# Attention scores of two heads in the two row halves of TensorE, and one operand split for a whole pair

## The chip, the cores and the metric

The kernel runs on one core of one Trainium2 chip. Its time is device microseconds of one execution. The program is one launch: all inputs lie in the chip's memory, and the output goes back there.

## What is computed

Two layers of a decoder trunk over 256 tokens of width 1024, in float32. Each layer first mixes: 12 self-attention heads and 4 heads that attend to 256 memory tokens, all of width 64, share one input projection and one output projection. Layer 0 adds a learned forgetting term to the scores, layer 1 a distance term. Then each layer runs a gated feed-forward block of 2816 columns.

```
for i in range(DEPTH):                       # DEPTH = 2
    xn = rms_norm(h, norm_mix[i]);  mn = rms_norm(mem, norm_mem[i])
    mk, mv = split(mn @ w_mem_kv[i])
    q, k, v, (f_logit), qm = split(xn @ w_in[i])
    self_out = softmax(q k^T / 8 + bias, causal) v      # 12 heads
    mem_out  = softmax(qm mk^T / 8) mv                  # 4 heads
    h = h + concat(self_out, mem_out) @ w_out[i]
    gu = rms_norm(h, norm_ffn[i]) @ w_gate_up[i]
    h = h + (silu(gu[..., :D_FF]) * gu[..., D_FF:]) @ w_down[i]
return rms_norm(h, norm_final)
```

With 256 tokens the block-sparse attention of layer 1 has a single block, so it is plain causal attention there.

## The kernel before

**Products.** Every float32 operand of a product is split into two parts, `hi` (a copy rounded to the matmul's input type, by ScalarE) and `lo` (what the copy lost, a subtraction by VectorE). A product of two such operands is three matmuls: hi·hi, lo·hi and hi·lo (`prod`, line 320). The weights come from memory as one stream of units on SyncE's queue; `split` (line 215) makes `hi` and `lo` of each half unit, a copy of 128x1024 on ScalarE (L227) and a subtraction on VectorE (L230), five half units ahead of their use, into seven buffers of each.

**The mixer** (line 470) computes the values of all heads, then three groups of query and key columns (`qk_ps`, two pairs of heads in each), with the memory heads' projection (`qm_ps`, and in layer 0 also the memory keys and values) ahead of the second group. A pair of heads is one tile of 128 partitions: head 0 in partitions 0 to 63, head 1 in 64 to 127 (`HOME`). Each pair's attention is a generator (`attend`, line 394), and `step` (line 464) moves all active ones on by a stage between pieces of projection: scores (`s_s`, or `s_m` for memory heads), softmax, transposes of the probabilities (`pT`), and the product with the values (`o_s`, `o_m`). TensorE and SyncE run in the order in which this is written. VectorE, ScalarE and GpSimd are ordered by a scheduler, in which the softmax has a raised priority (`URGENT`).

**Scores before.** A head has 64 rows only, so the two parts of an operand are stacked in the 128 rows. `split_queries` (line 378) writes for head a its `hi` into the head's own 64 partitions and its `lo` into the other 64. `split_keys` (line 386) writes `hi` of the keys into both halves, and `lo` into the own half, with zeros in the other (`no_lo`, line 334, on GpSimd). One matmul then gives hi·hi + lo·hi and a second hi·lo. So there are two matmuls of 256 columns for each head and each block of 128 queries, 8 for a pair. The cost is in the preparation: for a self pair 6 copies of 64x256 on ScalarE (L381, L389, L390), 2 subtractions on GpSimd and 2 on VectorE (L383, L392), and 2 zero fills. For two memory pairs the keys take 8 copies and 4 subtractions, and the queries 4 and 4. Of the two heads of a pair GpSimd subtracts for head 0 and VectorE for head 1.

**Softmax.** The maxima read the scores in their PSUM bank (L420 for memory heads, L417 for self heads, which writes the biased scores into the tile `p_s`), ScalarE takes the exponentials (L427; for memory heads straight from the bank, so the bank stays taken until then), VectorE the reciprocals and the scaling (L428, L431). The probabilities and their transposes share one tag of three buffers, `probs`. PSUM has eight banks, all of one tag.

**The value products** `o_s` and `o_m` (line 446) write head 0 to output partitions 0 to 63 and head 1 to 64 to 127: each head uses one half of TensorE's columns. They run in plain float32.

Of the kernel before, what the change touches and what calls it, by code (L numbers as in the profile page):

```python
# [141 lines left out]
def trunk(ctx: ExitStack, tc: tile.TileContext, plan, stream, x, gains, norm_final, square, mem, out):  # L142
# [23 lines left out]
    mem_t = [ap.tile([P, 2, 512], F32, tag="probs", name=f"mem{t}", bufs=3).rearrange("p a s -> p (a s)") for t in range(NT)]  # L166
# [176 lines left out]
    def mem_kv(i):  # L343
# [24 lines left out]
        for p in range(HM // 2):  # L368
            split_keys(mks[p], mk[:, p])
# [6 lines left out]
    ENG = (nc.gpsimd, nc.vector)  # L376

    def split_queries(dst, q):

        for a in range(2):  # L380
            nc.scalar.activation(dst[HOME[a], a], q[HOME[a]], AF.Copy)  # L381
        for a in range(2):
            r = ENG[a].tensor_sub(dst[HOME[1 - a], a], q[HOME[a]], dst[HOME[a], a].bitcast(F32))  # L383
        return r

    def split_keys(dst, k):

        for a in range(2):
            nc.scalar.activation(dst[HOME[a], a, :S], k[HOME[a]], AF.Copy)  # L389
            nc.scalar.activation(dst[HOME[1 - a], a, :S], k[HOME[a]], AF.Copy)  # L390
        for a in range(2):
            ENG[a].tensor_sub(dst[HOME[a], a, S:], k[HOME[a]], dst[HOME[a], a, :S].bitcast(F32))  # L392

    def attend(name, xq, xk, vt, h0, idle, bias, dst, kt):
# [10 lines left out]
        for a in range(2):  # L405
# [5 lines left out]
        pr = ap.tile([P, 2, 512], F32, tag="probs", name=f"p_{name}", bufs=3)  # L411
# [27 lines left out]
        pT = ap.tile([P, 2, 512], F32, tag="probs", name=f"pT_{name}", bufs=3)  # L439
# [30 lines left out]
    def mixer(i, xs, rs):  # L470
# [76 lines left out]
        def memory_heads():  # L547
# [15 lines left out]
            nc.vector.tensor_mul(qm, qb.t.rearrange("p (a s) -> p a s", a=2), rsb[:, 0:1, :].to_broadcast([P, 2, S]))  # L563
            for p in range(HM // 2):
                xq = ap.tile([P, 2, S], F32R, tag="work", name=f"xqm{i}{p}", bufs=WORK_BUFS)
                mem_done[i] = split_queries(xq, qm[:, p]).ins
                active.append(attend(f"m{i}{p}", xq, mks[p], mvs, 2 * p, IDLE_MEM[i] + p, None, hT, 6 + p))

        for g in range(3):
# [18 lines left out]
            for a in range(2):  # L588
# [9 lines left out]
                active.append(attend(f"s{i}{p}", xq, xk, vsb, 2 * p, idle, bias, hT, p))  # L598
# [46 lines left out]
    def ffn(i, xs, late):  # L645
# [5 lines left out]
        def gu(c, kk):  # L651
# [13 lines left out]
            if first:  # L665
                rsb.append(spread(rs, f"f{i}", (1.0,), "f")[:, 0])
# [156 lines left out]
```

## Time and profile before

| | us |
|---|---|
| median of 3 runs | 621.79 (621.36 to 622.78) |
| the profiled execution | 621.42 |
| its span | 619.6 |
| TensorE busy in the span | 606.8 |
| VectorE busy | 452.7 |
| ScalarE busy | 393.2 |
| GpSimd busy | 63.4 |

The granted clock of TensorE was 0.998 of full speed over the span. The span is the part of an execution between its first and last instruction; some 1.8 us lie around it. The profile has one line for nearly every matmul, since all of them are issued by one helper (L183), so matmuls are told apart by the tile they write. A matmul's record lasts longer than the distance to the next one's start, because they are pipelined: what a matmul costs is read from start to start.

### The profile page before, as it was taken

What the parts mean: (1) busy time and instruction counts of PE and PEld (TensorE: products, weight loads), DVE (VectorE), ACT (ScalarE), POOL (GpSimd) and SP (SyncE); (2) the same over time, 40 slices, a digit from 0 to 9 for tenths busy, and PEclk for the clock granted to TensorE, in tenths of its full rate; (3) what the DMA queues carried; (4) which work ended last, traced back from release to release, by engine and by line L of the source; (5) the groups of instructions that cost most, each with busy time, mean ns of one, the idle gap of its engine ahead of it and who ended that gap; (6) DMA issues with size and microseconds to landing.
All of it is one profiled execution on the core that took longest, in us unless ns stands there. A gap on an engine that the chain in (4) does not pass through costs nothing.

```text
span 619.6 us, 9546 instructions
## 1 busy us (share of the span) xinstructions
PE 606.8 (98%) x3634; PEld 533.0 (86%) x3634; DVE 452.7 (73%) x815; ACT 393.2 (63%) x736; POOL 63.4 (10%) x90
## 2 busy tenths in 40 slices
PE   9999899999999999999999999999999999999995
PEld 6999888788888888888899998877888888888884
DVE  5677999687676776668675589986866766667664
ACT  6889788485555555557467589776755555555542
POOL 2032112055000000000011032110000000000000
PEclk9999999999999999999999999999999999999999
DMA  8977452335544554556355731332445555456301
GB/s 349 422 283 278 165 179 95 135 137 204 199 172 179 197 204 181 177 190 227 126 200 191 272 137 69 136 136 103 170 177 197 205 195 178 177 197 205 136 1 68
DMA packets 16774, 112.31 MB, mean 181 GB/s; under 512 B 1996, under 2 KB 2008, under 8 KB 4312
## 3 DMA queue, kind: packets, MB, share of 16 engines
q1 hardware_dynamic: 16440, 111.42, 49.0%
q8 instruction: 28, 0.46, 0.3%
q10 hardware_dynamic: 288, 0.29, 0.1%
q14 instruction: 18, 0.15, 0.1%
HBM read 110.64 MB, written 1.06 MB: 180 GB/s over the span
## 4 chain that ended last, share of the span: by engine, by line
PE 88%; DVE 5%; ACT 4%; issue 2%; POOL 0%; POOLq 0%; DVEq 0%; ACTq 0%
PE gu L183 40%; PE d_acc L183 18%; PE qk_ps L183 8%; PE o_acc L183 7%; PE v_ps L183 6%; DVE lo L230 2%; PE s_s L183 1%; ACT hi L227 1%; PE pT_s L438 1%; PE o_s L183 1%; PE mv_ps L183 1%; PE qm_ps L183 1%; PE mk_ps L183 1%; PE warm_ps L183 1%; DVE p_m L431 1%
## 5 line engine op out<-in xcount | busy, mean ns | idle before, releaser
L230 DVE TENSOR_TENSOR lo<-raw,hi 128x1024 fp32r<-128x1024 f32 (+3 forms) x201 | 239.7, 1198 | 67.0 <-ACT hi L227 62.1
L227 ACT ACTIVATE hi<-raw 128x1024 fp32r<-128x1024 f32 (+3 forms) x201 | 206.5, 1035 | 71.3 <-PE d_acc L183 46.8
L183 PE MATMUL gu<-x_ffn,hi 128*128 128x512 f32 x704 | 177.4, 392 | 0.0
L183 PEld LDWEIGHTS gu<-x_ffn,hi 128*128 128x128 f32 x704 | 126.3, 189 | 22.2
L183 PE MATMUL d_acc<-hi,h 128*128 128x512 f32 x348 | 107.1, 389 | 0.0
L183 PEld LDWEIGHTS gu<-x_ffn,lo 128*128 128x128 f32 x704 | 96.7, 190 | 8.1 <-ACT x_ffn L251 1.0
L183 PE MATMUL gu<-x_ffn,lo 128*128 128x256 f32 x704 | 100.5, 284 | 0.1
L183 PEld LDWEIGHTS d_acc<-hi,h 128*128 128x128 f32 x348 | 65.3, 188 | 13.6
L183 PE MATMUL qk_ps<-x_x,hi 128*128 128x256 f32 x384 | 72.4, 284 | 2.1 <-ACT p_m L427 2.1
L183 PE MATMUL d_acc<-lo,h 128*128 128x512 f32 x174 | 67.7, 389 | 0.0
L183 PEld LDWEIGHTS qk_ps<-x_x,hi 128*128 128x128 f32 x384 | 61.0, 191 | 3.3 <-ACT p_m L427 2.5
L183 PE MATMUL qk_ps<-x_x,lo 128*128 128x256 f32 x192 | 54.3, 283 | 0.0
L672 ACT ACTIVATE gate<-gu 128x256 f32<-128x256 f32 x44 | 16.9, 384 | 57.6 <-PE gu L183 57.6
L672 ACT ACTIVATE up<-gu 128x256 f32<-128x256 f32 x44 | 16.9, 385 | 39.7 <-PE gu L183 39.5
L183 PE MATMUL o_acc<-hi,x_hT 128*128 128x512 f32 x128 | 41.6, 404 | 0.3 <-DVE x_hT L249 0.3
L183 PEld LDWEIGHTS d_acc<-lo,h 128*128 128x128 f32 x174 | 32.7, 188 | 6.8
L673 DVE TENSOR_TENSOR gate<-gu,gate 128x256 f32<-128x256 f32 x44 | 18.7, 424 | 25.6 <-ACT gate L672 25.5
L183 PEld LDWEIGHTS qk_ps<-x_x,lo 128*128 128x128 f32 x192 | 36.8, 191 | 0.0
L673 DVE TENSOR_TENSOR up<-gu,up 128x256 f32<-128x256 f32 x44 | 18.7, 424 | 24.6 <-ACT up L672 24.6
L183 PE MATMUL v_ps<-hi,x_x 128*128 128x384 f32 (+1 forms) x128 | 33.1, 339 | 0.0
L183 PEld LDWEIGHTS o_acc<-hi,x_hT 128*128 128x128 f32 x128 | 22.9, 188 | 5.9 <-DVE x_hT L249 1.0
L427 ACT ACTIVATE p_s<-p_s,nmax_s 128x128 f32<-128x128 f32 (+1 forms) x48 | 21.3, 445 | 9.8 <-DVE nmax_s L417 9.7
(152 smaller groups left out, 752.2 us busy)
## 6 DMA issues: line engine op xcount, KB each, us to landing
raw<-in_stream SPq DMA_DIRECT2D x94, 1024.0 KB, 4.8
raw<-in_stream SPq DMA_DIRECT2D x3, 1036.0 KB, 7.9
raw<-in_stream SPq DMA_DIRECT2D x4, 768.0 KB, 4.5
fk<-fd SPq DMA_DIRECT2D x3, 512.0 KB, 7.5
raw<-in_stream SPq DMA_DIRECT2D x2, 518.0 KB, 4.4
h<-in_x SPq DMA_DIRECT2D x2, 512.0 KB, 11.9
mem<-in_mem SPq DMA_DIRECT2D x2, 512.0 KB, 12.5
gfin<-in_norm_final SPq DMA_DIRECT2D x1, 512.0 KB, 3.6
```

Source lines behind the costliest of these rows:

```text
L183: nc.tensor.matmul(o, lhsT, rhs, start=self.fresh, stop=stop, skip_group_check=True)
L227: nc.scalar.activation(hi[:, c0:c1], src[:, c0:c1], AF.Copy)
L230: nc.vector.tensor_sub(lo[:, c0:c1], src[:, c0:c1], hi[:, c0:c1].bitcast(F32))
L427: nc.scalar.activation(pr[:, a, c], src, AF.Exp, bias=nmax[:, a, j], scale=scale, accum_out=total[:, a, j])
L431: nc.vector.tensor_scalar_mul(pr[:, a, c], pr[:, a, c], rc[:, a, qt:qt + 1])
L438: nc.tensor.transpose(tb[a].t[:, n * P:(n + 1) * P], pr[:, a, c:c + P], ident)
L672: nc.scalar.activation(v[:, 1], b[s].t[:, S:], AF.Copy)
L673: nc.vector.tensor_add(v[:, 0], b[s].t[:, :S], v[:, 1])
```

## The change

**Scores.** The query and key operands of a pair are now one `hi` tile and one `lo` tile of all 128 partitions, each head in its own 64. Three matmuls (hi·hi, lo·hi, hi·lo) for each head and block of queries take the head's 64 partitions alone, so each uses one half of TensorE's rows; the two heads stand alternately, and write to two banks. A pair has 12 matmuls of 256 columns where it had 8.

**Splits.** `split_queries`, `split_keys` and `no_lo` are gone. `split_ps` does a self pair's queries and keys together: one copy of 128x512 on ScalarE (L248) and one subtraction of 128x512 on VectorE (L249), into a tile `xp`. The two memory pairs' queries (`xm`) and keys (`mks`) take one copy and one subtraction each. GpSimd has no part in them.

**Buffers.** `probs` has four buffers instead of three. `xm` takes a buffer of the tag `pair` where the `xqm` tiles were in `work`. The feed-forward's spread of the norm factors shares the tag of the mixer's.

```diff
-    mem_t = [ap.tile([P, 2, 512], F32, tag="probs", name=f"mem{t}", bufs=3)...
+    mem_t = [ap.tile([P, 2, 512], F32, tag="probs", name=f"mem{t}", bufs=4)...
@@ split_ps
-            nc.vector.tensor_sub(lo, ps, hi.bitcast(F32))
+            return nc.vector.tensor_sub(lo, ps, hi.bitcast(F32))
@@
-    mks = [cp.tile([P, 2, 2 * S], F32R, name=f"mk{p}") for p in range(HM // 2)]
+    mks = cp.tile([P, 2, HM // 2, S], F32R, name="mks")
@@ mem_kv
-        for p in range(HM // 2):
-            split_keys(mks[p], mk[:, p])
+        split_ps(mks[:, 0], mks[:, 1], mk)
@@ removed: no_lo, ENG, split_queries, split_keys
@@ attend
-        for a in range(2):
-            for qt in range(NT):
-                o, q = sb[a].t[:, qt * S:(qt + 1) * S], slice(qt * P, (qt + 1) * P)
-                sb[a].mm(o, xq[:, a, q], xk[:, a, :S])
-                sb[a].mm(o, xq[:, a, q], xk[:, a, S:], stop=True)
+        for qt in range(NT):
+            o, q = slice(qt * S, (qt + 1) * S), slice(qt * P, (qt + 1) * P)
+            for n, (st, mv) in enumerate(((xq[0], xk[0]), (xq[1], xk[0]), (xq[0], xk[1]))):
+                for a in range(2):
+                    sb[a].mm(sb[a].t[:, o], st[HOME[a], q], mv[HOME[a]], stop=n == 2)
@@ attend: pr and pT
-..., tag="probs", ..., bufs=3)
+..., tag="probs", ..., bufs=4)
@@ memory_heads
+            xm = ap.tile([P, 2, HM // 2, S], F32R, tag="pair", name=f"xm{i}", bufs=PAIR_BUFS)
+            mem_done[i] = split_ps(xm[:, 0], xm[:, 1], qm).ins
             for p in range(HM // 2):
-                xq = ap.tile([P, 2, S], F32R, tag="work", name=f"xqm{i}{p}", bufs=WORK_BUFS)
-                mem_done[i] = split_queries(xq, qm[:, p]).ins
@@ mixer
-                xq = ap.tile([P, 2, S], F32R, tag="work", name=f"xq{i}{p}", bufs=WORK_BUFS)
-                xk = ap.tile([P, 2, 2 * S], F32R, tag="pair", name=f"xk{i}{p}", bufs=PAIR_BUFS)
-                no_lo(xk)
-                split_queries(xq, qk[:, 0])
-                split_keys(xk, qk[:, 1])
+                xp = ap.tile([P, 2, 2, S], F32R, tag="pair", name=f"xp{i}{p}", bufs=PAIR_BUFS)
+                split_ps(xp[:, 0], xp[:, 1], qk)
@@ ffn
-                rsb.append(spread(rs, f"f{i}", (1.0,), "f")[:, 0])
+                rsb.append(spread(rs, f"f{i}", (1.0,), "x")[:, 0])
```

**Where it moves instructions.** TensorE's order of blocks is the same in both kernels: each block of scores stands between the same neighbours. On ScalarE in layer 0, from the memory keys to the memory queries, before (`mk_87` is the second memory pair's keys, `xqm_742` and `xqm_747` the two pairs' queries, `hi` the weights' copies):

```order
L389 ACTIVATE mk_87<-mk_662 64x256
L390 ACTIVATE mk_87<-mk_662 64x256
L389 ACTIVATE mk_87<-mk_662 64x256
L390 ACTIVATE mk_87<-mk_662 64x256
L227 ACTIVATE hi_0_712<-raw_432 128x1024
L227 ACTIVATE hi_2_754<-raw_432 128x1024
L227 ACTIVATE hi_0_784<-raw_555 128x1024
L381 ACTIVATE xqm_742<-qm_740 64x256 x2
L381 ACTIVATE xqm_747<-qm_740 64x256 x2
```

and after (`mks` is the copy of all memory keys, `xm` that of all memory queries):

```order
L227 ACTIVATE hi_0_675<-raw_427 128x1024
L248 ACTIVATE mks<-mk_635 128x512
L227 ACTIVATE hi_2_710<-raw_427 128x1024
L227 ACTIVATE hi_0_740<-raw_528 128x1024
L248 ACTIVATE xm_705<-qm_703 128x512
L227 ACTIVATE hi_2_800<-raw_528 128x1024
L227 ACTIVATE hi_0_897<-raw_600 128x1024
```

The copies of small tiles between the weights' copies have become one for the keys and one for the queries, and one weights' copy more stands ahead of the keys.

On VectorE in layer 0, from the last weights' subtraction ahead of the memory queries to the first memory pair's maxima, before:

```order
L230 TENSOR_TENSOR lo_0_713<-raw_432,hi_0_712 128x1024
L563 TENSOR_TENSOR qm_740<-qm_ps_681,rsb_x_479 128x512
L230 TENSOR_TENSOR lo_2_755<-raw_432,hi_2_754 128x1024
L383 TENSOR_TENSOR xqm_742<-qm_740,xqm_742 64x256
L383 TENSOR_TENSOR xqm_747<-qm_740,xqm_747 64x256
L230 TENSOR_TENSOR lo_0_785<-raw_555,hi_0_784 128x1024
L230 TENSOR_TENSOR lo_2_841<-raw_555,hi_2_840 128x1024
L539 TENSOR_TENSOR bias_868<-fk,sq 128x256
L539 TENSOR_TENSOR fk<-fk,sq 128x2x128 x2
L420 TENSOR_REDUCE nmax_m_822<-s_m_0_812 128x1 x2
L420 TENSOR_REDUCE nmax_m_822<-s_m_1_813 128x1 x2
```

and after:

```order
L230 TENSOR_TENSOR lo_2_711<-raw_427,hi_2_710 128x1024
L540 TENSOR_TENSOR qm_703<-qm_ps_644,rsb_x_474 128x512
L230 TENSOR_TENSOR lo_0_741<-raw_528,hi_0_740 128x1024
L249 TENSOR_TENSOR xm_705<-qm_703,xm_705 128x512
L230 TENSOR_TENSOR lo_2_801<-raw_528,hi_2_800 128x1024
L516 TENSOR_TENSOR bias_828<-fk,sq 128x256
L516 TENSOR_TENSOR fk<-fk,sq 128x2x128 x4
L230 TENSOR_TENSOR lo_0_898<-raw_600,hi_0_897 128x1024
L397 TENSOR_REDUCE nmax_m_782<-s_m_0_768 128x1 x2
L397 TENSOR_REDUCE nmax_m_782<-s_m_1_769 128x1 x2
```

The two `xqm` subtractions have become one of `xm`. The weights' subtractions stand one place earlier throughout (`lo_2_711` of after is `lo_2_755` of before, and so on), so that the one of `raw_627`, the next row of before, which followed the maxima, is now ahead of them (`lo_0_898`), with four mask additions (`fk`) instead of two.

On VectorE in layer 1, the scaling of the second memory pair's probabilities (`p_m`, L431 before, L408 after), which the transposes `pT_m` wait for, before:

```order
L428 RECIPROCAL rc_m_3996<-total_m_3995 128x2
L591 TENSOR_TENSOR qk_4078<-qk_ps_3835,rsb_x_3729 128x512
L431 TENSOR_SCALAR p_m_3990<-p_m_3990,rc_m_3996 128x256 x2
L428 RECIPROCAL rc_m_3996<-total_m_3995 128x2
L230 TENSOR_TENSOR lo_1_4113<-raw_3696,hi_1_4112 128x1024
L431 TENSOR_SCALAR p_m_3990<-p_m_3990,rc_m_3996 128x256 x2
L417 ISA p_s_4048,nmax_s_4047<-s_s_0_4037,fk 128x128
L417 ISA nmax_s_4047 128x1
L417 ISA p_s_4048,nmax_s_4047<-s_s_0_4037,fk 128x256
```

and after:

```order
L405 RECIPROCAL rc_m_3913<-total_m_3912 128x2
L394 ISA p_s_3969,nmax_s_3968<-s_s_0_3954,fk 128x128
L394 ISA nmax_s_3968 128x1
L408 TENSOR_SCALAR p_m_3907<-p_m_3907,rc_m_3913 128x256 x2
L394 ISA p_s_3969,nmax_s_3968<-s_s_0_3954,fk 128x256
L394 ISA nmax_s_3968 128x1
L394 ISA p_s_3969,nmax_s_3968<-s_s_1_3955,fk 128x128
L394 ISA nmax_s_3968 128x1
L405 RECIPROCAL rc_m_3913<-total_m_3912 128x2
L394 ISA p_s_3969,nmax_s_3968<-s_s_1_3955,fk 128x256
L394 ISA nmax_s_3968 128x1
L408 TENSOR_SCALAR p_m_3907<-p_m_3907,rc_m_3913 128x256 x2
```

Before, a weights' subtraction stood between the two scalings of `p_m`; now the four biased maxima of the next self pair (`p_s`) stand between and ahead of them, and the weights' subtraction has gone to another place.

## Rows read from the trace of the kernel before

**Rows 1.** The page's line of busy times: microseconds, share of the span and number of instructions of each engine.

```profile
PE 606.8 (98%) x3634; PEld 533.0 (86%) x3634; DVE 452.7 (73%) x815; ACT 393.2 (63%) x736; POOL 63.4 (10%) x90
```

**Rows 2.** TensorE's timeline around its four long waits in the mixers, two rows each: start, us, the instruction, how many are merged, and in brackets the idle time before it with what ended it.

```profile
60.03 0.28 PE L183 MATMUL qk_ps<-x_x,hi 128*128 128x256 f32 x1
61.16 0.51 PE L183 MATMUL s_m<-mk,xqm 128*128 128x256 f32 x2 [0.85 <-POOL xqm L383]
...
71.25 0.61 PE L438 MATMUL pT_m<-sq,p_m 128*128 128x128 f32 x4
73.04 0.38 PE L183 MATMUL qk_ps<-x_x,hi 128*128 128x256 f32 x1 [1.18 <-ACT p_m L427]
...
73.74 0.28 PE L183 MATMUL qk_ps<-x_x,hi 128*128 128x256 f32 x1
74.89 0.39 PE L183 MATMUL qk_ps<-x_x,hi 128*128 128x256 f32 x1 [0.88 <-ACT p_m L427]
...
377.44 0.60 PE L438 MATMUL pT_m<-sq,p_m 128*128 128x128 f32 x4
379.18 0.63 PE L438 MATMUL pT_m<-sq,p_m 128*128 128x128 f32 x4 [1.14 <-DVE nmax_s L417]
```

**Rows 3.** Busy time by stretch. Columns: stretch and its length, then busy us (and instructions) of PE, PEld, DVE, ACT and POOL, the granted clock, DMA share and GB/s. The stretches: layer 0 from the first pairs' split to the end of the memory queries' projection, layer 0 from the first scores to the last long wait, layer 1 likewise.

```profile
36.60:54.40 17.80, 17.80 (x148) 17.21 (x147) 14.40 (x17) 16.55 (x30) 5.02 (x5) 1.00 0.57 214
...
60.20:75.00 14.80, 11.90 (x96) 11.32 (x96) 14.74 (x46) 10.48 (x31) 3.01 (x6) 1.00 0.58 224
...
364.20:379.60 15.40, 14.27 (x122) 14.06 (x121) 15.22 (x48) 12.98 (x39) 3.50 (x7) 1.00 0.44 159
```

**Rows 4.** The chain that ended last, in order of time (start, us, engine and line), in layer 0 from 55 to 75 us and in layer 1 around 376 us.

```profile
55.59 0.42 ACT mk L389
...
56.47 1.07 ACT hi L227
...
57.56 1.23 DVE lo L230
58.79 0.60 DVE qm L563
...
60.55 0.72 DVE xqm L383
...
65.67 1.33 DVE nmax_m L420 x4
67.00 1.13 DVE lo L230
...
73.86 0.99 ACT p_m L427 x4
...
375.81 0.97 DVE lo L230
...
376.86 1.62 DVE p_m L431 x2
```

**Rows 5.** Groups by line, shapes kept apart: busy us, mean ns of one, idle before. The last row is from the view of the tile `p_m`: shortest, median and longest ns of one.

```profile
L381 ACT ACTIVATE xq<-qk 64x256 fp32r<-64x256 f32 x24 | 10.0, 415 | 4.1 <-DVE qk L591 3.7
L389 ACT ACTIVATE xk<-qk 64x256 fp32r<-64x256 f32 x24 | 10.0, 416 | 0.4
L383 DVE TENSOR_TENSOR xq<-qk,xq 64x256 fp32r<-64x256 f32 x12 | 8.1, 678 | 1.5 <-ACT xq L381 1.2
L392 DVE TENSOR_TENSOR xk<-qk,xk 64x256 fp32r<-64x256 f32 x12 | 5.8, 481 | 1.2 <-ACT xk L389 0.9
L383 DVE TENSOR_TENSOR xqm<-qm,xqm 64x256 fp32r<-64x256 f32 x4 | 3.4, 896 | 0.1
L591 DVE TENSOR_TENSOR qk<-qk_ps,rsb_x 128x512 f32<-128x512 f32 x12 | 8.0, 679 | 1.6 <-ACT rsb_x L283 1.6
L442 ACT ACTIVATE pT_m<-pT_m 128x512 f32<-128x512 f32 x4 | 2.3, 576 | 0.0
L431 DVE TENSOR_SCALAR p_m<-p_m,rc_m x16: 333/350/873, 68.4 to 377.6; 128x256 f32<-128x256 f32 x16
```

**Rows 6.** The same chain where it runs through TensorE without a wait in layer 0: start, us, tile, matmuls. The rows at 82.73 and 92.31 follow a block of `o_m` or `o_s`, the other two don't.

```profile
78.19 2.87 PE qk_ps L183 x24
...
82.73 3.07 PE qk_ps L183 x24
...
92.31 1.14 PE s_s L183 x8
...
101.27 0.95 PE s_s L183 x8
```

**Rows 7.** TensorE's timeline around `F_ps` (a float32 product in one tile: four records, two of 256 columns and two of 128) and around one `o_m` block (eight records of 256 columns, four for each head). `128*128`, `128*12`, `128*64` are the rows and columns of the array in use.

```profile
41.39 0.28 PE L183 MATMUL mv_ps<-lo,x_mem 128*128 128x256 f32 x1
41.60 0.82 PE L183 MATMUL F_ps<-sq,lf 128*12 128x256 f32 x4
42.35 0.38 PE L183 MATMUL mk_ps<-x_mem,hi 128*128 128x256 f32 x1
...
81.64 0.44 PE L183 MATMUL o_m<-pT_m,mv 128*64 128x256 f32 x2
...
82.66 0.39 PE L183 MATMUL qk_ps<-x_x,hi 128*128 128x256 f32 x1
82.89 0.28 PE L183 MATMUL qk_ps<-x_x,lo 128*128 128x256 f32 x1
```

More of the change, by code (lines that the diff above doesn't have):

```diff
@@ L163, in trunk @@
     nc.gpsimd.memset(minus_half, -0.5)
-    mem_t = [ap.tile([P, 2, 512], F32, tag="probs", name=f"mem{t}", bufs=3).rearrange("p a s -> p (a s)") for t in range(NT)]
+    mem_t = [ap.tile([P, 2, 512], F32, tag="probs", name=f"mem{t}", bufs=4).rearrange("p a s -> p (a s)") for t in range(NT)]
     def load_x():
@@ L373, in mem_kv @@
         yield
[L376 to L392, printed above, removed]
     def attend(name, xq, xk, vt, h0, idle, bias, dst, kt):
@@ L404, in attend @@
         sb = [bank(f"s_{name}_{a}") for a in range(2)]
-        for a in range(2):
-            for qt in range(NT):
-                o, q = sb[a].t[:, qt * S:(qt + 1) * S], slice(qt * P, (qt + 1) * P)
-                sb[a].mm(o, xq[:, a, q], xk[:, a, :S])
-                sb[a].mm(o, xq[:, a, q], xk[:, a, S:], stop=True)
+        for qt in range(NT):
[3 more added lines that the diff above has]
+                    sb[a].mm(sb[a].t[:, o], st[HOME[a], q], mv[HOME[a]], stop=n == 2)
         nmax = sp.tile([P, 2, NT], F32, tag="nmax", name=f"nmax_{name}")
-        pr = ap.tile([P, 2, 512], F32, tag="probs", name=f"p_{name}", bufs=3)
+        pr = ap.tile([P, 2, 512], F32, tag="probs", name=f"p_{name}", bufs=4)
         with tc.high_priority(offset=URGENT):
@@ L438, in attend @@
                 nc.tensor.transpose(tb[a].t[:, n * P:(n + 1) * P], pr[:, a, c:c + P], ident)
-        pT = ap.tile([P, 2, 512], F32, tag="probs", name=f"pT_{name}", bufs=3)
+        pT = ap.tile([P, 2, 512], F32, tag="probs", name=f"pT_{name}", bufs=4)
         width = len(blocks) * P
@@ L563, in memory_heads @@
             nc.vector.tensor_mul(qm, qb.t.rearrange("p (a s) -> p a s", a=2), rsb[:, 0:1, :].to_broadcast([P, 2, S]))
+            xm = ap.tile([P, 2, HM // 2, S], F32R, tag="pair", name=f"xm{i}", bufs=PAIR_BUFS)
+            mem_done[i] = split_ps(xm[:, 0], xm[:, 1], qm).ins
             for p in range(HM // 2):
-                xq = ap.tile([P, 2, S], F32R, tag="work", name=f"xqm{i}{p}", bufs=WORK_BUFS)
-                mem_done[i] = split_queries(xq, qm[:, p]).ins
-                active.append(attend(f"m{i}{p}", xq, mks[p], mvs, 2 * p, IDLE_MEM[i] + p, None, hT, 6 + p))
+                active.append(attend(f"m{i}{p}", (xm[:, 0, p], xm[:, 1, p]), (mks[:, 0, p], mks[:, 1, p]), mvs, 2 * p,
+                                     IDLE_MEM[i] + p, None, hT, 6 + p))
         for g in range(3):
@@ L591, in mixer @@
                 nc.vector.tensor_mul(qk.rearrange("p a s -> p (a s)"), kb[a].t, rsb.rearrange("p a s -> p (a s)"))
-                xq = ap.tile([P, 2, S], F32R, tag="work", name=f"xq{i}{p}", bufs=WORK_BUFS)
-                xk = ap.tile([P, 2, 2 * S], F32R, tag="pair", name=f"xk{i}{p}", bufs=PAIR_BUFS)
-                no_lo(xk)
-                split_queries(xq, qk[:, 0])
-                split_keys(xk, qk[:, 1])
+                xp = ap.tile([P, 2, 2, S], F32R, tag="pair", name=f"xp{i}{p}", bufs=PAIR_BUFS)
+                split_ps(xp[:, 0], xp[:, 1], qk)
                 idle = a + IDLE[i][g]
-                active.append(attend(f"s{i}{p}", xq, xk, vsb, 2 * p, idle, bias, hT, p))
+                active.append(attend(f"s{i}{p}", (xp[:, 0, 0], xp[:, 1, 0]), (xp[:, 0, 1], xp[:, 1, 1]), vsb, 2 * p, idle, bias, hT, p))
         acc = [[bank(f"o_acc{i}{t}{c}") for c in range(2)] for t in range(NT)]
@@ L772, in trunk @@
         nc.gpsimd.memset(warm, 0.0)
-        for mk in mks:
-            no_lo(mk)
         wb = bank("warm_ps")
```

2 lines of the change are left out of this document (removed).

## The prediction

> **What bounds the kernel now.** I read the busy line first: TensorE works in 98% of the span, the next engine, VectorE, in 73% [rows 1]. So what changes TensorE's stream, or its waits, changes the time; work taken from other engines counts only where TensorE waits for it. Next come TensorE's waits. In both mixers together it waits long four times, and from start to start each costs a little more than the bracket says: in layer 0 the scores `s_m` start 1.13 us after the matmul before, where 0.12 is usual, a loss of 1.0; the projection after `pT_m` starts 1.8 us after a group of four transposes that takes 0.44, a loss of 1.35; its next bank costs 1.15 − 0.12 = 1.03; in layer 1 the second half of `pT_m` starts 1.74 after the first, a loss of 1.3 [rows 2]. Sum 4.7 us. Behind them, by the stretches, is VectorE: busy 14.74 of 14.80 us in layer 0 and 15.22 of 15.40 in layer 1, while before that, from 36.6 to 54.4, ScalarE is the fuller one, 16.55 of 17.80 [rows 3]. The chain says the same: the small copies of the memory keys (L389) end at 56.45 and hold the weights' copy behind them, that one holds the weights' subtraction, that one `qm`, and then `xqm` and the maxima follow on VectorE without a gap [rows 4].
>
> **The change on TensorE, matmuls.** A block of scores of one pair takes 0.95 us for 8 matmuls, 0.12 each [rows 6]. Now there are 12. If the two row halves run side by side, they are six steps of 0.12: 0.72 us, 0.23 less; over 16 pairs 3.7 us gained. If one half waits for the other, they are 1.44 us, 0.49 more, over 16 pairs 7.8 us lost. No row shows row halves. The nearest are column halves: `F_ps`, in one tile, needs 0.75 us from its first start to the next tile's first for 768 columns, of which some 0.2 is leaving the tile, so about 0.18 for 256 columns; the `o_m` block, in two halves of the columns, brings 2048 columns in 1.02 us, 0.13 for 256 with its switches, and its first two records lie in 0.44 us together [rows 7]. One after the other they would need over 1.4. So halves of the array do run side by side here, with two loads of weights, and I take that for the rows.
>
> **The change on TensorE, switches.** Column halves show a price too. The projection's 24 matmuls take 2.87 us after a full-array block and 3.07 after `o_m`; the scores 0.95 and 1.14 [rows 6]: 0.20 us for coming back. Part of it is the first matmul, which lasts 0.39 instead of 0.28 since nothing hides its weights' load [rows 7]. Going in costs similarly: from the last full matmul to `F_ps` 0.21 instead of 0.12 [rows 7], and the first load uncovered. I take 0.2 either way. Counted in TensorE's order, which the change leaves as it is: of the 8 blocks of scores in a layer, two touch each other, one has column halves on both sides, two more on one side. Where column halves were beside full-array scores, a switch was paid already. What is new is 4 ways in and 6 ways out in each layer, 20 in all, so 4.0 us lost. The bounds are 0 (row halves with all 128 columns might need no switch) and 20 x 0.25 = 5. I take 0.2 since no row gives a reason why rows should switch more cheaply than columns.
> The sum on TensorE is then +0.3 us: the change's own matmuls pay for their switches and no more.
> The Trainium skill's "TensorEngine Tiling (Array Packing)", section Tiling Modes, states that changing the tiling mode drains TensorE; that speaks against this change, and the rows at column halves agree with it (0.2 us), none shows row halves. By that rule the switches cost what I took; without it the forecast would be 4 us lower.
>
> **The change on the other engines.** Counted for a self pair: ScalarE loses six copies of 0.416 and gains one of 128x512, for which the nearest row is 0.576: −1.9 us. VectorE loses subtractions of 0.68 and 0.48 and gains one of 128x512, 0.68: −0.5 us. For the two memory pairs' queries ScalarE goes from 4 x 0.416 to 0.58, VectorE from 2 x 0.896 to 0.68 (−1.1); for the keys ScalarE from 8 x 0.416 to 0.58 (−2.7) [rows 5]. GpSimd loses all of its part, and VectorE is rid of a neighbour: two scalings of `p_m` took 1.62 us together in layer 1 where 0.35 each is the median and 0.873 the longest [rows 4, 5]. Almost all of it hides behind TensorE and counts for nothing; where it counts are the four waits.
> *First wait.* Up to the memory queries ScalarE is spared 2 x 1.9 + 2.7 = 6.5 us, so it is no longer late at 54.4, when the queries' projection ends. From there: `qm` 0.7, copy 0.58, a weights' subtraction 1.2, `xm` 0.7, together 3.2, so 57.6; TensorE wants it at 60.15. The wait of 1.0 goes, with 2.5 us to spare.
> *Second and third wait.* They end when the second memory pair's exponentials free two PSUM banks, at 73.0 and 74.9. Behind the first maxima (65.6) lay a weights' subtraction of 1.13 [rows 4], which now stands ahead of them. With seven buffers it takes one that TensorE frees at about 60.15; then ScalarE copies for 1.07, so it ends at 62.4 and the maxima start 3.2 us earlier than before. The banks come free 3.2 + 1.1 earlier, at 68.7 and 70.6. TensorE, without its first wait and with 0.3 of switches, wants them at 60.15 + 10.53 (from 61.16 to 71.25 + 0.44 [rows 2]) + 0.3 = 71.0 and 71.7. Both waits go, with 1 us to spare; if they stay in part, they cost up to 2.4.
> *Fourth wait.* The weights' subtraction between the two scalings (0.97 in the chain) has gone, the scalings shrink from 1.62 to about 0.7, `xm` saves 1.1 before; four biased maxima, about 1.1, have come ahead. That is 1.9 earlier against a wait of 1.3 and 0.3 of switches: it goes, narrowly.
> What is late next would be weights; but the code makes them five half units ahead of their use (`split`), so I cost a weights' subtraction that moves by one place at nothing. The fourth `probs` buffer I cost at nothing, either way: no long wait of TensorE ends on it. The feed-forward's shared factor tile, too: its last reader is done long before.
>
> **The sum.** 621.42 − 4.7 + 0.3 = 617.0 against the profiled execution; the median lies 0.37 above that, so **617.4**.
>
> **The rivals.**
> *Halves one after the other (slower).* If the row halves share a path (the weights' load, or the way to PSUM) a pair of half matmuls takes two steps. 16 x 0.49 = 7.8 instead of −3.7: 617.4 + 11.5 = 628.9; if only the loads follow each other, at 0.11 us each (the first matmul's 0.39 less 0.28 [rows 7]), six steps of 0.22 make 1.3 a pair and the time is 626.9. It decides against the change once two half matmuls take more than 0.17 us: 16 x (6 x 0.17 − 0.95) = 1.1, plus 4.0 of switches, is what the waits give back. Against it stand the column halves; for it, that no row shows rows. Chance 0.21.
> *Halves overlap in part.* Steps of 0.16 make a pair 0.96, no gain, and the switches 4.0 stand against 4.7 of waits: 621.1. Or the halves are as forecast, and 3 us of the waits only move, to the banks or to the weights: 620.4. Chance together 0.15. The skill's "TensorE: Matmul & The Clock Gate", Part 3, gives 3.07 times for four row tiles, less than full overlap; by that figure I would estimate steps near this case.
> *No switch for rows.* Then the gain of 3.7 stands in full: 617.4 − 4.0 = 613.4. Nothing shows it; it would need TensorE to keep its stream from full rows to halves. Chance 0.12.
> *It doesn't do what it says* is the first rival in its extreme, so it has no chance of its own.
>
> **How the numbers follow.** Forecast 617.4 (616 to 619), chance 0.52. The range leaves out the slow end of the first rival and the tail under the third: 613.2 to 627. A measurement of this kernel can tell about 0.2%, 1.2 us, from no change. Faster than 620.5: 0.52 + 0.12 and a quarter of the mixed case, 0.68; within: most of the mixed case, 0.10; slower: the first rival and a little of the mixed one, 0.22.
>
> **What would show it.** Score blocks in the chain: 0.73 us for 12 matmuls, records of the two heads starting in pairs some ns apart and the pairs 0.12 apart (right), all 0.12 apart (first rival). A full-array block after scores 0.2 longer than elsewhere (switch) or not. No waits near 60, 72, 74 and 378 us, and VectorE under 98% in those stretches. Wrong would be: a new wait of over 1 us in a mixer, or a time outside 613 to 627.

## The result and the profile after

| | before | after |
|---|---|---|
| median, runs made together | 622.28 us (621.36 to 622.92) | 617.07 us (616.86 to 617.21) |
| the profiled execution | 621.42 | 617.18 |
| its span | 619.6 | 615.4 |

The ratio is 0.992, 95% interval 0.9908 to 0.9933: the change gains 0.8%, 5 us. The forecast was 617.4. Executions of the kernel before come in two groups, near 621.5 and near 623 us (more of this under `copies_apart`); against the first group the gain is some 4.5 us.

The page's line of busy times of after, against [rows 1]:

```profile
PE 606.4 (99%) x3698; PEld 530.2 (86%) x3698; DVE 442.6 (72%) x799; ACT 363.4 (59%) x656; POOL 24.2 (4%) x30
```

TensorE has 64 matmuls more (4 for each of 16 pairs) and is busy as long as before, 606.4 us against 606.8. The span is 4.2 us shorter, so the gain is idle time of TensorE that has gone, not work that became cheaper. ScalarE does 30 us less and GpSimd 39 us less, most of which nobody waited for. The view of TensorE's waits of after says the same (us in total, times, longest): all that it lists is the start of the program and two short waits of the output projection.

```profile
PE warm_ps L183 <- POOL warm L747: 1.3, 1, 1.3
PE o_acc L183 <- DVE x_hT L249: 0.3, 2, 0.2
```

Busy time of after in the stretches of [rows 3], with the same columns:

```profile
36.60:54.40 17.80, 17.80 (x147) 17.21 (x147) 15.78 (x17) 14.32 (x20) 0.00 (x0) 1.00 0.79 278
60.20:75.00 14.80, 14.80 (x143) 14.00 (x141) 14.67 (x57) 11.34 (x35) 0.00 (x0) 1.00 0.31 118
364.20:379.60 15.40, 15.27 (x141) 14.20 (x141) 14.65 (x54) 13.24 (x41) 0.00 (x0) 1.00 0.22 81
```

TensorE is busy 14.80 of 14.80 us where it was 11.90. ScalarE ahead of it fell from 16.55 to 14.32. VectorE is as full as before, 14.67 of 14.80: it now does 57 instructions there instead of 46, and TensorE no longer stands in step with it.

TensorE's timeline of after at the first scores of the memory heads, where it had lost 1.0 us [rows 2]:

```profile
60.47 0.28 PE L183 MATMUL qk_ps<-x_x,hi 128*128 128x256 f32 x1
60.68 0.96 PE L183 MATMUL s_m<-mks,xm 64*128 64x256 f32 x12
```

and VectorE's timeline of after, where the operand `xm` of those scores is made:

```profile
57.32 0.68 DVE L249 TENSOR_TENSOR xm<-qm,xm 128x512 fp32r<-128x512 f32 x1
```

ScalarE's copy ahead of it, in ScalarE's timeline of after:

```profile
56.05 0.61 ACT L248 ACTIVATE xm<-qm 128x512 fp32r<-128x512 f32 x1
```

`xm` is ready at 58.0, 2.7 us ahead of the first score at 60.68. Before, the memory queries' subtraction started at 60.55 [rows 4].

The chain of after, through TensorE without a wait (start, us, tile, matmuls), against [rows 6]:

```profile
60.75 0.90 PE s_m L183 x12
61.65 3.06 PE qk_ps L183 x24
64.70 0.91 PE s_s L183 x12
65.61 0.70 PE s_m L183 x12
...
71.30 2.87 PE qk_ps L183 x24
```

Here both prices can be read, from the end of one block to the end of the next. The 12 matmuls of a pair that follows another pair's scores take 0.70 us, six steps of 0.117, where 8 took 0.95. The same 12 behind a full-array block take 0.90 or 0.91, and the projection behind scores takes 3.06 where it takes 2.87 behind transposes: a change of tiling costs 0.20 us on the way in and 0.19 on the way out.

A group by line of after, ScalarE's copy for a self pair (busy us, mean ns of one), and the tile `p_m` (shortest, median, longest ns of one), against [rows 5]:

```profile
L248 ACT ACTIVATE xp<-qk 128x512 fp32r<-128x512 f32 x12 | 7.3, 626 | 2.1 <-DVE qk L569 2.1
L408 DVE TENSOR_SCALAR p_m<-p_m,rc_m x16: 341/348/356, 65.3 to 374.2; 128x256 f32<-128x256 f32 x16
```

### The profile page after: what moved, and what is told of

It is laid out like the page before. It is cut to its first block, busy times and chain, and to the rows that moved or that the text cites. A ratio compares the mean times of both kernels' runs of the same rounds, so it can differ in the third digit from the quotient of the medians.

```text
span 615.4 us, 9466 instructions
## 1 busy us (share of the span) xinstructions
PE 606.4 (99%) x3698; PEld 530.2 (86%) x3698; DVE 442.6 (72%) x799; ACT 363.4 (59%) x656; POOL 24.2 (4%) x30
## 4 chain that ended last, share of the span: by engine, by line
PE 95%; DVE 2%; ACT 1%; issue 0%; POOLq 0%; POOL 0%; ACTq 0%
PE gu L183 40%; PE d_acc L183 19%; PE qk_ps L183 11%; PE o_acc L183 7%; PE v_ps L183 6%; PE mk_ps L183 2%; PE qm_ps L183 2%; PE mv_ps L183 2%; PE s_s L183 1%; PE pT_s L415 1%; PE o_s L183 1%; PE warm_ps L183 1%; DVE lo L230 1%; PE o_m L183 1%; ACT hi L227 0%; PE pT_m L415 0%
## 5 line engine op out<-in xcount | busy, mean ns | idle before, releaser
L230 DVE TENSOR_TENSOR lo<-raw,hi 128x1024 fp32r<-128x1024 f32 (+3 forms) x201 | 239.5, 1198 | 70.4 <-ACT hi L227 65.3
```

Of the source, the lines that this page charges most:

```text
L230: nc.vector.tensor_sub(lo[:, c0:c1], src[:, c0:c1], hi[:, c0:c1].bitcast(F32))
```

## The experiments

All are edits of the changed kernel, and each was compared with the kernel before on the same chip.

| run | median, us | ratio to before, 95% interval |
|---|---|---|
| `full_rows` | 616.80 | 0.9906 to 0.9933 |
| `old_split` | 624.37 | 1.0027 to 1.0052 |
| `same_half` | 628.15 | 1.0084 to 1.0112 |
| `probs3` | 617.04 | 0.9909 to 0.9934 |
| `old_copies` | 622.80 | 1.0001 to 1.0019 |
| `old_subs` | 617.66 | 0.9911 to 0.9936 |
| `by_head` | 621.70 | 0.9986 to 1.0003 |
| `merge_m` | 616.47 | 0.9892 to 0.9920 |
| `copies_apart` | 622.70 | 1.0005 to 1.0022 |
| `half_copies` | 616.95 | 0.9907 to 0.9934 |

### The two parts apart: new splits with full-array scores, and old splits with row halves

`full_rows` keeps the new splits and leaves out the row halves. With them it leaves out the third product and the separation of the two heads, so it prices the time alone:

```diff
-        for qt in range(NT):
-            o, q = slice(qt * S, (qt + 1) * S), slice(qt * P, (qt + 1) * P)
-            for n, (st, mv) in enumerate(((xq[0], xk[0]), (xq[1], xk[0]), (xq[0], xk[1]))):
-                for a in range(2):
-                    sb[a].mm(sb[a].t[:, o], st[HOME[a], q], mv[HOME[a]], stop=n == 2)
+        for a in range(2):
+            for qt in range(NT):
+                o, q = slice(qt * S, (qt + 1) * S), slice(qt * P, (qt + 1) * P)
+                sb[a].mm(sb[a].t[:, o], xq[0][:, q], xk[0])
+                sb[a].mm(sb[a].t[:, o], xq[1][:, q], xk[0], stop=True)
```

> The changed kernel's splits, buffers and order, but the scores as 8 full-array matmuls of 128 rows for a pair (hi of the queries with hi of the keys, then lo with hi), so no tiling switch and no row halves. Part of the computation is changed: a score is then the sum over both heads of the pair, and the hi-lo product is left out. Theory (the four waits carry the gain, the row halves pay only for their own switches): the score blocks with what they add to their neighbours take as long as before, so 617.0 us, within 0.5 of the changed kernel, and no long wait of TensorE in the mixers. Rival (the side-by-side matmuls carry the gain): they are gone, so 3.7 us of the gain go with them, 620.8.

Measured: 616.80, which theory gave and the rival (620.8) did not. Its chain:

```profile
64.16 0.96 PE s_s L183 x8
```

So the row halves contribute nothing to the gain: with blocks of 8 full-array matmuls of 0.96 us the median is 0.3 us below that with 12 half ones, and the executions of the two overlap. All of the 5 us comes with the new splits.

`old_split` is the other part alone: row halves, with the old small copies and subtractions.

```diff
+    def split_small(hi, lo, src, keys):
+        for a in range(2):
+            nc.scalar.activation(hi[HOME[a]], src[HOME[a]], AF.Copy)
+            if keys:
+                nc.scalar.activation(spare[HOME[1 - a]], src[HOME[a]], AF.Copy)
+        for a in range(2):
+            r = ENG[a].tensor_sub(lo[HOME[a]], src[HOME[a]], hi[HOME[a]].bitcast(F32))
+        return r
...
-                split_ps(xp[:, 0], xp[:, 1], qk)
+                for j in range(2):
+                    split_small(xp[:, 0, j], xp[:, 1, j], qk[:, j], j == 1)
```

> The changed kernel's scores in row halves and its four probability buffers, but the work of the split as it was: 64x256 copies on ScalarE, with the second copy of the keys' hi written to a spare tile, and 64x256 subtractions, head 0 on GpSimd and head 1 on VectorE. The zero fills are not brought back. Theory (the waits carry the gain): most of the four waits, 4.7 us, are back, so 621.5 (620.3 to 622.5), with waits near 60, 72, 74 and 378 us. Rival (the side-by-side matmuls carry it): 617.1 to 618.0.

Measured: 624.37, 2.9 us above theory and outside its range. The waits are back, as its view of TensorE's waits shows:

```profile
PE qk_ps L183 <- ACT p_m L418: 3.4, 3, 1.7
...
PE s_m L183 <- POOL xm L345: 0.4, 1, 0.4
```

They are longer than before's: four in layer 0, from start to start together 4.2 us longer than in after, and one in layer 1, 1.5 longer. In its profiled execution TensorE's clock fell too, which I had not thought of; it is told under `copies_apart`, and it explains little of the median.

### Whether the halves run at once

`same_half` puts both heads on the first half of the rows, so that nothing can run side by side.

```diff
-                    sb[a].mm(sb[a].t[:, o], st[HOME[a], q], mv[HOME[a]], stop=n == 2)
+                    sb[a].mm(sb[a].t[:, o], st[HOME[0], q], mv[HOME[0]], stop=n == 2)
```

> The changed kernel with both heads' scores on the first row half, still alternating between two banks, so that no two can run side by side. Part of the computation is changed: head 1 of a pair gets the scores of head 0. This prices the rival that the halves run one after the other. A block of 12 then takes 1.4 us instead of 0.70, 16 times: 11.2 us, so 628.3 us. If the 12 are no slower on one half (the steps are set by something else, such as issue), 617 us.

Measured: 628.15. Its chain:

```profile
65.17 1.62 PE s_s L183 x12
66.79 1.42 PE s_m L183 x12
```

1.42 us against 0.70: two half-array matmuls take one step on two halves and two steps on one. The slow rival of the prediction, 628.9, is what this kernel is.

`by_head` gives the program six matmuls of head 0 and then six of head 1, on their own halves.

```diff
-        for qt in range(NT):
-            o, q = slice(qt * S, (qt + 1) * S), slice(qt * P, (qt + 1) * P)
-            for n, (st, mv) in enumerate(((xq[0], xk[0]), (xq[1], xk[0]), (xq[0], xk[1]))):
-                for a in range(2):
+        for a in range(2):
+            for qt in range(NT):
+                o, q = slice(qt * S, (qt + 1) * S), slice(qt * P, (qt + 1) * P)
+                for n, (st, mv) in enumerate(((xq[0], xk[0]), (xq[1], xk[0]), (xq[0], xk[1]))):
                     sb[a].mm(sb[a].t[:, o], st[HOME[a], q], mv[HOME[a]], stop=n == 2)
```

> The changed kernel with a pair's scores written head by head: six matmuls of head 0, then six of head 1, instead of alternately. Theory A (TensorE keeps the two halves going by itself, as with the value products, whose two heads are written one after the other and yet start in pairs): 617.1, with records in pairs some ns apart. Theory B (only neighbours in the order overlap): eleven steps instead of six, 5 x 0.115 x 16 = 9.2 us more, 626.3.

Measured: 621.70, neither. The matmuls of `s_m` that are in flight in the first stretches of its first block (stretch, length, busy and number, then the granted clock and the DMA's columns):

```profile
60.84:60.95 0.11, 0.10 (x1) 1.00 1.41 596
...
61.18:61.30 0.12, 0.12 (x5) 1.00 1.45 614
```

and the same view of after at its first block:

```profile
60.67:60.72 0.05, 0.04 (x2) 1.00 1.16 492
```

In after two matmuls are in flight from the first 50 ns. In `by_head` one half works alone at first; from 61.18 on, three steps later, new matmuls start on both. The chain of `by_head` at that block:

```profile
60.91 1.24 PE s_m L183 x12
```

and its timeline of TensorE where scores of a self pair and of a memory pair follow each other:

```profile
65.97 0.27 PE L183 MATMUL s_m<-mks,xm 64*128 64x256 f32 x1
66.08 0.28 PE L183 MATMUL s_s<-xp 64*128 64x256 f32 x1
...
66.20 0.28 PE L183 MATMUL s_s<-xp 64*128 64x256 f32 x1
```

A matmul of `s_m` starts at 65.97, ahead of two matmuls of `s_s` that stand before it in the program. TensorE thus starts a matmul of the other half ahead of its turn, but only some three matmuls ahead: a block takes 1.24 us instead of 0.90. Two blocks that touch lose this once, so it makes 14 x 0.34 = 4.8 us, about the 4.6 that the run lost. The alternating order of the change is needed. The Trainium skill's "TensorE: Matmul & The Clock Gate", Part 3, section The mechanism, says that matmuls start strictly in program order; this timeline shows otherwise between two row halves.

### The fourth buffer

`probs3` gives `probs` three buffers again (three places of `bufs=4` to `bufs=3`).

```diff
-        pr = ap.tile([P, 2, 512], F32, tag="probs", name=f"p_{name}", bufs=4)
+        pr = ap.tile([P, 2, 512], F32, tag="probs", name=f"p_{name}", bufs=3)
```

> The changed kernel with three probability buffers instead of four. Theory: no long wait of TensorE ended on that buffer, so 617.1 us, within 0.6. Rival (the fourth buffer is what lets the softmax run ahead and ends the waits): the second, third and fourth wait come back, 620.7.

Measured: 617.04 against 617.07. The fourth buffer makes no difference that can be measured.

### Which engine's relief it is

`old_copies` puts back ScalarE's small copies and keeps one subtraction of 128x512 on VectorE:

```diff
+                for j in range(2):
+                    split_small(xp[:, 0, j], xp[:, 1, j], qk[:, j], j == 1)
+                nc.vector.tensor_sub(xp[:, 1], qk, xp[:, 0].bitcast(F32))
```

> The changed kernel, but ScalarE's copies as they were (64x256, the keys' second one to a spare tile); one subtraction of 128x512 on VectorE and none on GpSimd. Theory (the three waits of layer 0 come from ScalarE being late with the splits and the weights' copies behind them, the fourth from VectorE): the waits of layer 0, 3.4 us, are back and the fourth is not, 620.5 (619.5 to 621.5). Rival (GpSimd beside VectorE is what made the waits): 617.1 to 617.8.

`old_subs` puts back the small subtractions on GpSimd and VectorE and keeps ScalarE's one copy:

```diff
+                nc.scalar.activation(xp[:, 0], qk, AF.Copy)
+                for j in range(2):
+                    split_small(xp[:, 0, j], xp[:, 1, j], qk[:, j], j == 1)
```

> The changed kernel, but the subtractions as they were (64x256, head 0 on GpSimd and head 1 on VectorE); ScalarE has its one copy. Theory (ScalarE for layer 0, VectorE for the fourth wait): the fourth wait and a part of the first are back, 618.7 (617.8 to 619.7). Rival (GpSimd beside VectorE made the waits): all are back, 621 to 624.

Measured: 622.80 and 617.66. ScalarE's copies alone take back 5.7 us, the subtractions 0.6. Both miss the ranges of their theories, the first by 1.3 us upwards, the second by 0.1 downwards. GpSimd beside VectorE is out as the cause: it is back in `old_subs`, and the waits are not. The views of TensorE's waits of the two:

```profile
PE s_m L183 <- DVE xm L556: 1.6, 1, 1.6
...
PE qk_ps L183 <- ACT p_m L416: 1.3, 1, 1.3
```

```profile
PE qk_ps L183 <- ACT p_m L415: 0.2, 1, 0.2
```

ScalarE's timeline of `old_copies` ahead of the first wait:

```profile
56.49 0.42 ACT L343 ACTIVATE spare<-mk 64x256 fp32r<-64x256 f32 x1
56.93 2.95 ACT L227 ACTIVATE hi<-raw 128x1024 fp32r<-128x1024 f32 x3
59.88 1.74 ACT L341 ACTIVATE xm<-qm 64x256 fp32r<-64x256 f32 x4
```

It is the picture of before [rows 4]: the memory keys' copies run into 56.9, three weights' copies are queued behind them, and the queries' copies start at 59.9, where in after the one copy runs at 56.05. That the profile names VectorE's `xm` for the wait means only that VectorE is last in line.

### Why these runs lost more than the waits

`old_copies` was slower than theory by 2.3 us. Two explanations: its one subtraction must wait for all four copies, or something else was lost. Busy time by stretch of `old_copies`; the third column from the end is the granted clock:

```profile
61.00:62.00 1.00, 0.18 (x2) 0.00 (x0) 1.00 (x1) 0.95 (x3) 0.00 (x0) 1.00 1.05 442
...
64.00:65.00 1.00, 1.00 (x9) 1.00 (x8) 1.00 (x4) 0.00 (x0) 0.00 (x0) 0.76 1.06 451
65.00:66.00 1.00, 1.00 (x7) 1.00 (x7) 1.00 (x3) 0.00 (x0) 0.00 (x0) 0.50 1.01 377
66.00:67.00 1.00, 1.00 (x6) 1.00 (x6) 1.00 (x2) 0.00 (x0) 0.00 (x0) 0.50 1.07 451
67.00:68.00 1.00, 1.00 (x7) 0.99 (x5) 1.00 (x4) 0.53 (x3) 0.00 (x0) 0.53 0.95 401
```

TensorE waits from 60.9 to 62.8, works again, and then the granted clock falls to 0.50, 1.2 GHz, for some 3.2 us: 6 or 7 matmuls lie in a microsecond where 10 or 11 are usual. At these clocks the four stretches lose 0.24 + 0.50 + 0.50 + 0.47 = 1.7 us.

Only the first of the three waits of layer 0 is back in this execution, 1.9 us long. By the time TensorE reaches the place of the second and third, it is 3.5 us later than in after (the transposes start at 73.71 instead of 70.21), and there is no wait. So layer 0 is 3.8 us longer than in after, about the 3.4 of the theory, but by one wait and the clock. Layer 1 is 1.2 us longer, by a wait of 1.3 that ends at 376.60, and 0.9 us more lie at the end of the program, behind TensorE's last matmul.

`copies_apart` gives each pair its own subtraction, to shorten that wait:

```diff
-            mem_done[i] = nc.vector.tensor_sub(xm[:, 1], qm, xm[:, 0].bitcast(F32)).ins
+                mem_done[i] = nc.vector.tensor_sub(xm[:, 1, j], qm[:, j], xm[:, 0, j].bitcast(F32)).ins
```

> ScalarE's small copies as in the run before with old copies (622.8), but each pair gets its own subtraction of 128x256 on VectorE, so the first memory pair's scores no longer wait for all four copies of the queries. In the earlier run the granted clock fell to 0.50 from 64.5 to 67.7 us, right behind the wait of 1.86 at 60.8; at 64 to 68 that costs about 1.7 us (1 us at 0.76, two at 0.50, one at 0.53). Theory: ScalarE's copies bring back waits of the size of the kernel before, 3.5 to 4 us, and what old copies lost beyond that was the clock. Then the first wait shrinks to about 1.0 and the clock stays at 1.00: 622.8 - 0.85 - 1.7 = 620.3 (619.5 to 621.0). If the clock falls all the same: 622.0. Rival: the excess was not the clock, and the time is that of old copies less the shorter wait, 622.0, with the clock at 1.00.

Measured: 622.70 (622.13 to 623.15), 2.4 us above theory and 0.7 above the other two cases. The first wait shrank more than I had said, to 0.57 us (the group at 61.16 starts 0.69 after the one before it), but others came in its place, and the clock fell all the same, elsewhere. TensorE's timeline:

```profile
69.68 0.98 PE L183 MATMUL s_s<-xp 64*128 64x256 f32 x12
71.14 1.18 PE L427 MATMUL pT_m<-sq,p_m 128*128 128x128 f32 x8 [0.49 <-DVE nmax_s L406]
73.51 0.39 PE L183 MATMUL qk_ps<-x_x,hi 128*128 128x256 f32 x1 [1.18 <-ACT p_m L416]
...
75.03 0.39 PE L183 MATMUL qk_ps<-x_x,hi 128*128 128x256 f32 x1 [0.54 <-ACT p_m L416]
```

and its stretches behind them:

```profile
75.00:76.00 1.00, 0.97 (x6) 0.97 (x7) 1.00 (x6) 1.00 (x2) 0.00 (x0) 0.72 0.00 0
76.00:77.00 1.00, 1.00 (x6) 1.00 (x6) 1.00 (x6) 0.99 (x4) 0.00 (x0) 0.50 0.00 0
...
78.00:79.00 1.00, 1.00 (x7) 1.00 (x6) 0.90 (x3) 1.00 (x6) 0.00 (x0) 0.57 0.00 0
```

With 0.50 from 77 to 78 too, that is 0.28 + 0.50 + 0.50 + 0.43 = 1.7 us again. The waits, from start to start: 0.57 at the first; `pT_m` 1.46 after `s_s` where 0.91 is usual, 0.55; the projection 2.37 after eight transposes that take 0.85, 1.5; its next bank 0.82 after the matmul before it where 0.12 is usual, 0.7; and one of 1.28 by its bracket in layer 1, at 377.60, where after has one of 0.4. Sum 4.6, 4.2 more than in after, with the clock 5.9; the span is 6.0 us longer than after's. So in this execution some 1.7 us of what these copies cost is clock, and the rest waits. `old_split` has the same fall in its profiled execution (0.50 from 77 to 80). The kernel before has waits of about the same length, and in its profiled execution it kept its clock: 1.00 in the stretch that follows them.

```profile
75.00:80.00 5.00, 5.00 (x43) 5.00 (x44) 4.92 (x19) 4.86 (x16) 2.00 (x3) 1.00 0.00 0
```

That is not so in every execution. The mean granted clock of a whole execution is 0.994 or 0.995 in the three traces with the fall, and 0.996 to 0.998 in the others. Of the 47 executions of the kernel before that ran beside these experiments, 11 have 0.994 or 0.995 and take 622.75 to 623.40 us; the other 36 have 0.996 to 0.998 and take 621.22 to 621.98. So the kernel before most likely has the fall in a quarter of its executions, at a price of some 1.5 us; no trace of such an execution was kept. The changed kernel and the runs without long waits in the mixers (43 executions in all) are never under 0.996.

The same split shows what the fall costs in the end. In `copies_apart` five executions at 0.996 to 0.998 take 622.13 to 622.39 and five at 0.994 or 0.995 take 622.70 to 623.15 (one at 0.999, with 623.02, doesn't fit); in `old_split` three take 623.99 to 624.37 and two 624.58 and 624.99. Where the clock held, these kernels are thus only 0.6 to 0.8 us faster, and still 5 and 7 us slower than after: most of their excess over theory is not the clock. A slower TensorE meets fewer waits behind it, as `old_copies` shows above; that this makes the difference between 1.7 and 0.7 is likely, not shown. What `old_copies` would take without the fall no run tells, since 11 of its 12 executions lie at 0.993 or 0.994. When the clock falls and when it doesn't, the runs don't tell either.

### Load or deadline

`half_copies` adds to the changed kernel only the keys' second copies, into a tile that nobody reads.

```diff
+    def more_copies(src):
+        for a in range(2):
+            nc.scalar.activation(spare[HOME[1 - a]], src[HOME[a]], AF.Copy)
...
                 split_ps(xp[:, 0], xp[:, 1], qk)
+                more_copies(qk[:, 1])
```

> The changed kernel (617.07) with the keys' second copies put back on ScalarE alone, written to a tile that nobody reads: 4 more copies of 64x256 for the memory keys, 2 more for each self pair, 0.42 us each. Up to the memory queries that gives back 4 x 0.83 / 2 x ... = 2 pairs x 0.83 + 1.66 = 3.3 of the 6.5 us that ScalarE was spared. Theory of a deadline: the memory queries' split was ready 2.6 us ahead of its use (58.0 against 60.59), so the first wait is at most 0.7, the others stay away or nearly: 617.6 (617.1 to 618.4). Rival, that the time goes with ScalarE's load in proportion: half of the copies cost half of the 4 us, 619.1 (618.6 to 620).

Measured: 616.95, a little below the theory's range, so these copies cost nothing at all. The stretch ahead of the memory queries in `half_copies`, and then in `old_copies`:

```profile
36.60:54.40 17.80, 17.80 (x148) 17.21 (x147) 14.77 (x16) 16.27 (x26) 0.00 (x0) 1.00 0.67 246
```

```profile
36.60:54.40 17.80, 17.80 (x147) 17.21 (x147) 12.95 (x14) 16.57 (x30) 0.00 (x0) 1.00 0.60 208
```

ScalarE is busy 16.27 us in one and 16.57 in the other, and the times are 617 and 623. A busy share doesn't tell them apart; the start of the memory queries' copies does. In `half_copies` ScalarE even waits for them:

```profile
57.82 0.63 ACT L248 ACTIVATE xm<-qm 128x512 fp32r<-128x512 f32 x1 [0.94 <-DVE qm L549]
```

Their subtraction there starts at 58.83 and takes 0.69, so `xm` is ready at 59.5, still ahead of the scores at some 60.6. The gain is a deadline met, not time saved in proportion.

### Fewer changes of tiling

`merge_m` delays the memory pairs by one step: 42 changes of tiling instead of 50. Of the four that go in each layer, two go because another two blocks of scores touch, and two because a block of `o_m` now stands beside one of `o_s`.

```diff
-IDLE_MEM = (1, 1)
+IDLE_MEM = (2, 2)
```

> The changed kernel with the memory pairs one stage later (IDLE_MEM 2 instead of 1), so that their scores stand beside those of the first two self pairs, and two of the later ones beside column halves: 42 instead of 50 changes of tiling in TensorE's order. Theory (a change of tiling costs 0.2 us whatever its kind): 1.6 us less, 615.5, if no wait comes of it; two pairs' softmax at once may bring one back, then 616 to 618. Rival (leaving row halves costs, entering does not, or the reverse): 616.3 to 617.1 without any wait.

Measured: 616.47, 0.6 below the changed kernel (its span is 1.0 shorter, 614.4), where eight changes at 0.2 make 1.6. New waits stand against it, one on the second memory pair's banks in layer 0:

```profile
70.68 0.39 PE L183 MATMUL qk_ps<-x_x,hi 128*128 128x256 f32 x1 [0.16 <-ACT p_m L404]
```

and one inside that pair's transposes, here in layer 1:

```profile
377.14 1.34 PE L415 MATMUL pT_m<-sq,p_m 128*128 128x128 f32 x8
378.24 0.36 PE L183 MATMUL qk_ps<-x_x,hi 128*128 128x256 f32 x1
```

From the layer's first matmul of the query and key projection (`qk_ps`) to its last output projection matmul, layer 0 takes 98.17 us in both kernels. In it `merge_m` loses 0.4 us at the banks, from start to start, and 0.2 in the transposes. Layer 1 takes 84.99 instead of 85.68, 0.7 less; there the transposes take 1.10 us to the next start where the changed kernel's take 0.79, 0.3 lost, while a wait of 0.4 that the changed kernel has (below) is gone. So the four changes fewer are worth 0.6 us in either layer, about 0.15 each, three quarters of what the chain shows for one. This is the fastest of the kernels run, ahead of before by 0.8 to 1.1%.

## Why the prediction was right, and where not

**Matmuls, right.** Six steps of 0.12, 0.72 us: measured 0.70. `same_half` shows the alternative at 1.42.

**Changes of tiling, right.** 0.2 us either way: measured 0.20 and 0.19. The Trainium skill's "TensorEngine Tiling (Array Packing)", section Tiling Modes, says that a change of mode drains TensorE; the price of 0.2 us agrees with that for row halves too. The sum on TensorE, forecast as +0.3, is nearer to nothing, 16 x (0.70 − 0.95) + 20 x 0.2 = 0.0: layer 0, measured as above, takes 98.17 us in after and 98.23 in `full_rows`; layer 1 85.68 and 85.29, the difference being after's wait of 0.4.

**The four waits, right in sum.** 4.7 us were to go. They went; one of 0.4 us came in layer 1, where the first matmul of the projection starts 1.23 us after the first of eight transposes. At the same place in layer 0 it starts 0.85 us after:

```profile
370.44 1.09 PE L415 MATMUL pT_m<-sq,p_m 128*128 128x128 f32 x8
371.67 0.39 PE L183 MATMUL qk_ps<-x_x,hi 128*128 128x256 f32 x1
```

```profile
70.21 1.09 PE L415 MATMUL pT_m<-sq,p_m 128*128 128x128 f32 x8
71.06 0.37 PE L183 MATMUL qk_ps<-x_x,hi 128*128 128x256 f32 x1
```

−4.7 + 0.0 + 0.4 = −4.3. Measured from the layer's first `qk_ps` matmul to its last output projection matmul, layer 0 is 3.75 us shorter (101.92 to 98.17) and layer 1 0.94 (86.62 to 85.68), together 4.7; and in after's profiled execution the first of these matmuls starts 0.44 us later, at 24.23 instead of 23.79, which leaves the 4.2 of the span. That the forecast came so close to the time is in part luck: the sum on TensorE was 0.3 too high, and the new wait of 0.4 was not in it.

**The second and third wait, with less to spare than forecast.** The banks were to come free at 68.7 and 70.6, 4.3 us earlier than before. ScalarE's timeline of after, its last readings of the two banks:

```profile
70.19 0.20 ACT L404 ACTIVATION_READ_ACCUMULATOR p_m<-s_m,nmax_m 128x1 f32 x1
...
71.31 0.20 ACT L404 ACTIVATION_READ_ACCUMULATOR p_m<-s_m,nmax_m 128x1 f32 x1
```

They end at 70.4 and 71.5, 2.6 and 3.3 us earlier than before, and TensorE writes to the banks from 71.06 and 71.85: 0.7 and 0.3 us to spare, not 2.3 and 1.1. The wait of 0.4 in layer 1 is at the same place.

**The fourth wait, gone, but its cause is not shown.** The prediction gave it to VectorE: a weights' subtraction moved, the scalings rid of a GpSimd neighbour, `xm` 1.1 us cheaper. The scalings did shrink, from 0.873 at most to 0.356. But `old_subs` has the neighbour and the dear subtractions back, and its layer 1 takes 85.74 us against after's 85.68: these two did not make the wait. `old_copies` has neither and waits 1.3 us in that part of layer 1, but one block of the projection earlier, for the banks, where after has its 0.4. So ScalarE's copies cost time in layer 1 too; with TensorE held up there, the fourth wait can't show. No run brings it back at its own place, and no run moved a weights' subtraction alone, so what made it stays open.

**A sign that failed.** I had written that VectorE would fall under 98% in those stretches. In layer 1 it did, 14.65 of 15.40; in layer 0 it is at 14.67 of 14.80, 99%: freed of one thing it did the next, and so its busy share was no sign of TensorE's wait.

**Sizes.** ScalarE's copy of 128x512 costs 0.626, not 0.576. It changed nothing, since `xm` had 2.7 us to spare. The fourth `probs` buffer is worth nothing, as costed.

**The rivals.** Halves one after the other is what `same_half` measured, and the change is not that. The mixed case, with 3 us of the waits only moved, fell with after's list of waits. No switch for rows fell with the 0.20 us in the chain. The clock, which none of them named, would have belonged into a case where waits stay: by the executions of before, `copies_apart` and `old_split` it adds 0.6 to 1.5 us to them.

## What to carry to other kernels

Where one engine feeds another in a chain, ask when the last operand is ready against when it is wanted: copies that fit in the slack cost nothing, and about as many again cost some 6 us, in waits and in the clock that falls behind them. A change with two parts needs both apart on the chip: here the part that the title names first is worth nothing by itself, and the gain comes from the preparation that it allows. Whether that preparation can be had without row halves no run shows: `full_rows`, which tries it, adds the scores of two heads together. Where heads share TensorE by rows, alternate them in the program, and put blocks of one tiling next to each other.

## What the hardware showed that I had not expected

- Two 64-row matmuls of 256 columns on the two halves take one step, 0.117 us, with no measurable loss against a full-array matmul.
- TensorE starts matmuls of the other half out of program order, but only some three ahead: 1.24 us for a block written head by head, 0.90 alternating.
- Behind one wait of 1.9 us, or three of 0.55, 1.5 and 0.7 within 5 us, the granted clock fell to 0.50 for about 3.3 us, after TensorE had resumed, and those stretches lost 1.7 us. Behind the waits of the kernel before it did not in the traced execution; by their mean clock (0.994 or 0.995) and time, 11 of 47 others had a fall, at a price of some 1.5 us.
- Eight changes of tiling fewer, half of them of row halves and half of column halves, gave about 0.15 us each, a little less than the 0.2 that the chain shows for one.
